# Attention in a written order: filler behind each bank of transposes, scan behind the transposes, value difference by halves

## The chip, the cores and the metric

The kernel runs on one core of one Trainium2 chip. A core has a matrix engine (TensorE, PE in the profile, with its weight loads shown as PEld), a vector engine (VectorE, DVE), a scalar engine (ScalarE, ACT), a general engine (GpSimd, POOL) and a queue for transfers (SyncE, SP). Each engine runs its own list of instructions in order and waits on semaphores for the others. Matmul results land in PSUM banks; everything else is kept in on-chip tiles, and larger tensors are sent to and fetched from memory by DMA. The metric is the device time of one execution in microseconds (us), as the median of several runs.

## The reference

One layer of a trunk with a parallel mixer: an input projection gives queries, keys and values for 16 heads of 64 columns, a gated convolution and two gates; then an output projection and a SwiGLU feed-forward part. Batch 1, 1024 tokens, 1024 columns, all in float32. The part around which the change turns is the attention, which has no softmax: weights come from a product of "not taken" probabilities over later keys.

```python
def stick_breaking_attention(q, k, v):
    """A[t,s] = sigmoid(z_ts) * prod_{s<j<t} (1 - sigmoid(z_tj)),  z = q.k / sqrt(Dh), s < t."""
    ...
    for i in range(s_len // Q_BLOCK):
        t0 = i * Q_BLOCK
        n_keys = t0 + Q_BLOCK
        qb = qh[:, :, t0:t0 + Q_BLOCK]
        kp = kh[:, :, :n_keys]
        vp = vh[:, :, :n_keys]
        z = jnp.einsum('bhqd,bhkd->bhqk', qb, kp) * inv_sqrt
        ...
        log_not = jnp.where(mask, jax.nn.log_sigmoid(-z), 0.0)
        excl = lax.cumsum(log_not, axis=3, reverse=True) - log_not
        log_a = jax.nn.log_sigmoid(z) + excl
        a = jnp.where(mask, jnp.exp(log_a), 0.0)
        outs.append(jnp.einsum('bhqk,bhkd->bhqd', a, vp))
```

## The kernel before

**Arithmetic.** Each float32 operand is split into a high part (a copy rounded to the matmul's format, made by ScalarE) and a low part (the rest, made by a VectorE subtract), and a product is three matmuls: high by high, high by low, low by high. So a weight `raw` becomes `whi` and `wlo`.

**The stages.** Norm and modulation, then the projections for keys, values, queries, convolution and gates (to about 567 us), then the attention stage (about 567 to 1030 us), the branch and output projections, and the feed-forward part. Outside the attention stage the change moves next to nothing.

**One step of the attention.** There are 16 heads with 8 query blocks each, 128 steps (h, i); step i sees (i+1) x 128 keys. Per step:

1. Scores: two matmuls per 512 keys into a bank `z` (two banks; lines 798 and 799). ScalarE takes the sigmoid into the tile `pt` (line 800; five `pt` tiles).
2. VectorE runs one scan over `pt` (line 804), which turns the sigmoids into running products from the last key back: 128 x (i+1) columns in one instruction.
3. Two steps later TensorE transposes `pt` in 128 x 128 blocks, up to four in a bank `tr` (three banks; line 819). ScalarE copies the bank to `ath` (line 822), and VectorE subtracts to get the low part `atl` (line 823), which frees the bank. A weight is the difference of two neighbouring running products; the kernel takes that difference on the value side instead, as told below.
4. For each pair of query blocks, three steps behind, the "av" matmuls multiply `ath` and `atl` by `vt` into the bank `o` (lines 834 and 835). ScalarE copies one half (`otmp`, line 839), VectorE adds the other (`oy`, line 841), SP sends it to `d_ya`.

`vt` of a head holds the differences of neighbouring value rows: `vb` and `va` (two loads of the same values, one row apart, for a pair of heads, `load_v`, line 748) are subtracted in `att_dv`, and the difference of a head is split into high and low. There is one buffer each of `va` and `vb`, so that the next pair can be loaded only once the difference has been taken (`va`) and split (`vb`).

**Fillers.** Attention does not keep TensorE busy by itself. The generator `fillers` brings other matmuls: first the second half of the value projection (256 columns each, lines 911 to 913, results copied to `vs` by ScalarE and written to `d_v`), 16 chunks of 24 matmuls; then two series of 16 chunks of 24 matmuls of 512 columns for the convolution branch (lines 892 to 894, in banks `pj`, of which there are two). Their VectorE and ScalarE work (`cy`, `ybl`, `mb`, and the weight splits `whi` and `wlo`) is issued with them.

**What sets the order.** `attention` yields after each part with a number that says how much filler the part is worth, and a loop at the end of the stage (functions below) issues filler up to that share. The first sixteen half chunks (`HEAD`) are written ahead of the attention, with the value projection's first half in them. The attention is traced at high priority; a scheduler then places each engine's instructions by its own estimate of when they can run, and `issue_after` keeps a filler behind the last score matmul. So neither TensorE's order nor VectorE's is the one in which the code is written: instructions of different steps pass each other.

## Time and profile before

| What | us |
|---|---|
| Median of 3 runs | 1842.04 (1841.74 to 1842.79) |
| Profiled execution | 1840.08 |
| Its span | 1838.3 |
| TensorE busy in the span | 1803.6 |
| VectorE busy | 1353.5 |
| ScalarE busy | 792.3 |

The span is the time from the first to the last instruction of the profiled execution. A profile's row for a group of instructions gives line, engine, operation, output and inputs, the count, then busy time in us and the mean of one in ns, then the engine's idle time just ahead of them and who ended it. A row of the waits gives engine, line, tile and whom it waited for, then the sum in us, the number of times and the longest. A row of the timeline gives the start in us, the duration, the engine and the instruction, and in brackets the idle time before it. A row of the windows gives the length of the window and then the busy time with the number of instructions for PE, PEld, DVE, ACT and POOL; after these come the clock granted to TensorE (1.00 is full speed), the share of the DMA engines and GB/s. Matmul ends are modelled and overlap the next one's start, so starts are what to compare.

### The profile page before, as it was taken

How to read it: one execution, taken by the hardware profiler on the slowest of the kernel's cores; microseconds unless marked ns; L12 is line 12 of the kernel's file. 1: busy time of each engine (PE TensorE's matmuls, PEld its weight loads, DVE VectorE, ACT ScalarE, POOL GpSimd, SP SyncE). 2: the span in 40 equal slices, each digit the busy share in tenths (PEclk: the TensorE clock that was granted, in tenths of full speed). 3: DMA queues.
4: the chain of work that ended last, by engine and by line, in shares of the span. 5: the costliest groups of instructions: out<-in, count | busy, mean ns of one | idle time of the engine just before them, and what ended most of it. 6: DMA issues, size and time to landing. Idle time of an engine off the chain costs nothing.

```text
span 1838.3 us, 24895 instructions
## 1 busy us (share of the span) xinstructions
PE 1803.6 (98%) x8829; PEld 1501.9 (82%) x8829; DVE 1353.5 (74%) x1949; ACT 792.3 (43%) x1494; POOL 366.4 (20%) x277
## 2 busy tenths in 40 slices
PE   7999999999999999999999999999999999999999
PEld 4787778888889988888888788877888888878887
DVE  7873776779874888888887644589877788644776
ACT  3452553333343656665665311664444344422321
POOL 0043327423240000000000000105544454200000
PEclk9999999999999999999999999999999999999999
DMA  9598452217748566588544636424533344299766
GB/s 395 198 317 303 162 188 76 86 70 260 275 157 265 153 183 180 178 240 278 153 133 141 209 126 209 142 92 161 195 138 147 130 172 170 103 340 334 283 228 221
DMA packets 147267, 358.01 MB, mean 195 GB/s; under 512 B 15480, under 2 KB 44480, under 8 KB 144968
## 3 DMA queue, kind: packets, MB, share of 16 engines
q1 hardware_dynamic: 101816, 289.12, 46.3%
q10 hardware_dynamic: 44320, 63.64, 9.9%
q0 software_dynamic: 1008, 3.67, 0.5%
q8 instruction: 70, 1.15, 0.3%
q14 instruction: 53, 0.43, 0.1%
HBM read 245.74 MB, written 110.66 MB: 194 GB/s over the span
## 4 chain that ended last, share of the span: by engine, by line
PE 76%; DVE 11%; DMA 6%; issue 3%; ACT 3%; POOL 0%; ACTq 0%; SPq 0%; DVEq 0%; POOLq 0%
PE e L131 6%; PE e L132 6%; PE e L133 6%; PE pj L131 5%; PE pj L133 5%; PE pj L132 5%; PE pj L308 5%; PE pj L892 4%; PE pj L893 4%; PE pj L894 4%; PE e L1427 4%; PE e L1426 4%; PE e L1428 4%; PE tr L819 3%; PE o L835 2%
## 5 line engine op out<-in xcount | busy, mean ns | idle before, releaser
L804 DVE TENSOR_TENSOR_SCAN pt<-pt,mk 128x128 f32<-128x128 f32 (+7 forms) x128 | 172.1, 1350 | 48.8 <-ACT pt L800 48.6
L800 ACT ACTIVATE pt<-z,rq 128x512 f32<-128x512 f32 (+3 forms) x192 | 107.3, 580 | 88.9 <-PE z L799 57.4
L131 PE MATMUL e<-big,whi 128*128 128x512 f32 x352 | 137.7, 391 | 1.9 <-ACT c L1326 1.9
L133 PE MATMUL e<-big,wlo 128*128 128x512 f32 x352 | 137.7, 391 | 0.0
L132 PE MATMUL e<-big,whi 128*128 128x512 f32 x352 | 137.6, 391 | 0.0
L136 DVE TENSOR_TENSOR c<-e,c 128x512 f32<-128x512 f32 x138 | 93.0, 687 | 56.0 <-PE e L133 55.0
L122 POOL TENSOR_SCALAR rs_m<-ss 128x1 f32<-128x1 f32 x8 | 1.5, 192 | 651.8 <-ACT xn L1229 651.8
L131 PE MATMUL pj<-big,whi 128*128 128x512 f32 x320 | 125.1, 391 | 0.5 <-DVE c L136 0.4
L132 PE MATMUL pj<-big,whi 128*128 128x512 f32 x320 | 124.7, 390 | 0.0
L133 PE MATMUL pj<-big,wlo 128*128 128x512 f32 x320 | 124.4, 390 | 0.0
L1426 PE MATMUL e<-whi,f 128*128 128x512 f32 (+1 forms) x319 | 121.7, 382 | 1.6 <-DMA f<-d_f 1.6
L1427 PE MATMUL e<-wlo,f 128*128 128x512 f32 (+1 forms) x319 | 121.8, 382 | 0.0
L1428 PE MATMUL e<-whi,f 128*128 128x512 f32 (+1 forms) x319 | 121.6, 382 | 0.0
L136 DVE TENSOR_TENSOR c<-pj,c 128x512 f32<-128x512 f32 x140 | 93.2, 682 | 27.3 <-PE pj L133 26.4
L136 DVE TENSOR_TENSOR wlo<-raw,whi 128x512 fp32r<-128x512 f32 x116 | 88.1, 763 | 34.2 <-ACT whi L489 34.1
L308 PE MATMUL pj<-whi,big 128*128 128x512 f32 x352 | 109.4, 396 | 3.7 <-ACT big L291 3.6
L489 ACT ACTIVATE whi<-raw 128x512 fp32r<-128x512 f32 x116 | 72.7, 631 | 89.1 <-PE pj L132 38.8
L823 DVE TENSOR_TENSOR atl<-tr,ath 128x512 fp32r<-128x512 f32 (+1 forms) x192 | 99.6, 548 | 14.4 <-ACT ath L822 12.6
L136 POOL TENSOR_TENSOR ws<-raw,raw 128x512 f32<-128x512 f32 x40 | 55.4, 1384 | 273.6 <-DMA raw<-w_cg 165.2
L822 ACT ACTIVATE ath<-tr 128x512 fp32r<-128x512 f32 (+1 forms) x192 | 86.9, 490 | 44.8 <-PE o L834 26.0
L132 PE MATMUL e<-rl,whi 128*128 128x512 f32 x264 | 103.6, 392 | 2.5 <-DVE rl L136 2.5
L892 PE MATMUL pj<-big,whi 128*128 128x512 f32 x256 | 103.9, 406 | 0.0
(258 smaller groups left out, 5015.9 us busy)
## 6 DMA issues: line engine op xcount, KB each, us to landing
f<-d_f SPq DMA_DIRECT2D x77, 512.0 KB, 3.6
d_f<-fs SPq DMA_DIRECT2D x70, 512.0 KB, 3.2
raw<-w_cg SPq DMA_DIRECT2D x40, 512.0 KB, 4.4
raw<-w_u SPq DMA_DIRECT2D x26, 512.0 KB, 3.2
raw<-w_g SPq DMA_DIRECT2D x25, 512.0 KB, 3.4
ad<-ada ACTq DMA_DIRECT2D x19, 512.0 KB, 5.0
ada<-ada SPq DMA_DIRECT2D x8, 1024.0 KB, 9.6
d_t<-ts SPq DMA_DIRECT2D x16, 512.0 KB, 4.0
```

The source lines that it names most:

```text
L131: nc.tensor.matmul(ps, wh[:, k, :], fh[:, k, :], start=(k == 0), stop=False)
L132: nc.tensor.matmul(ps, wh[:, k, :], fl[:, k, :], start=False, stop=False)
L133: nc.tensor.matmul(ps, wl[:, k, :], fh[:, k, :], start=False, stop=(k == 3))
L136: eng.tensor_tensor(out=out, in0=a, in1=b, op=op)
L308: nc.tensor.matmul(ps, a, b, start=(k == 0 and q == 0), stop=(k == KT - 1 and q == 2))
L800: nc.scalar.activation(pt[:, off + s0:off + s0 + m], z[:, :m], AF.Sigmoid, scale=rq[:, 1, i, h:h + 1])
L804: nc.vector.tensor_tensor_scan(out=pt[:, rev], data0=pt[:, rev], data1=mk[:, rev], initial=1.0, op0=ALU.mult, op1=ALU.max)
L823: nc.vector.tensor_tensor(out=tl[:, :nb, c0:c0 + P], in0=src, in1=th[:, :nb, c0:c0 + P].bitcast(F32), op=ALU.subtract)
L892: nc.tensor.matmul(ps, wh, rh_, start=(k == 0), stop=False)
L1426: nc.tensor.matmul(o, sh, w[0][:, c], start=(j == 0), stop=False)
L1427: nc.tensor.matmul(o, sh, w[1][:, c], start=False, stop=False)
L1428: nc.tensor.matmul(o, sl, w[0][:, c], start=False, stop=(j == NJ - 1))
```

## The change

In words:

- The attention's own VectorE instructions and all TensorE instructions from the start of the attention loop to the end of the fillers are chained: each gets a dependency on the one before it on its engine that is for the order alone. They then run as written. ScalarE, GpSimd, SP and the fillers' VectorE work are still placed by the scheduler.
- The amounts of filler are three numbers: `F_Z` behind a part of the scores, `F_T` for each transposed block, `F_O` behind av. A bank of four transposes is followed by filler, and av by none. Filler comes in pieces of one `k` (three matmuls, `KQ` 1) instead of two.
- The scan leaves `att_scores` and is issued after the transposes of two steps earlier. The av of a pair comes last in its step, save where the pair's second block is block 5: there it comes between the two banks of transposes.
- The value difference is taken for 64 columns of a head at a time: sixteen subtracts of 128 x 8 x 64 instead of eight of 128 x 8 x 128, one in step 3 (4 for every other head), the split two steps later.

The counts of instructions stay the same on TensorE, ScalarE, GpSimd and SP; VectorE gets eight more.

```diff
+    F_Z, F_T, F_O = 0.2,0.3,0
...
-    def att_dv(h):
+    def att_dv(h, part):
         va, vb = vab["va"], vab["vb"]
-        if h % 2 == 0:
-            tt(nc.vector, vb, vb, va, ALU.subtract)
-        dv = vb[:, :, h % 2 * DH:h % 2 * DH + DH]
+        cs = slice(h % 2 * DH, h % 2 * DH + DH)
+        dv = vb[:, :, cs]
+        if part == 0:
+            tt(nc.vector, dv, dv, va[:, :, cs], ALU.subtract)
+            return
...
             if s0 + m < n:
-                yield m / 512 * 0.43
+                yield F_Z
+        yield F_Z
+
+    def att_scan(h, i):
+        pt, off = ptof[h, i], D - (i + 1) * P
         rev = slice(D - 1, off - 1 if off else None, -1)
         nc.vector.tensor_tensor_scan(out=pt[:, rev], data0=pt[:, rev], data1=mk[:, rev], initial=1.0,
                                      op0=ALU.mult, op1=ALU.max)
-        yield m / 512 * 0.43
...
-            yield nb * 0.11
+            yield F_T * nb
...
-        yield (2 * g + 2) * 0.22
-
-    NZ, NTR, NPJ, DAV, KQ = 2, 3, 2, 3, 2
+        yield F_O
+
+    NZ, NTR, NPJ, DAV, KQ = 2, 3, 2, 3, 1
...
-                    if s == 2:
-                        att_dv(0)
-                    if s % 8 == (6 if h % 2 else 5) and h + 1 < H:
-                        att_dv(h + 1)
+                    if s in (1, 2):
+                        att_dv(0, s - 1)
+                    if s % 8 in ((4, 6) if h % 2 else (3, 5)) and h + 1 < H:
+                        att_dv(h + 1, s % 8 // 5)
...
                 yield from att_scores(h, i)
-            if s >= DAV:
-                h, i = steps[s - DAV]
-                if s % 2 != DAV % 2:
-                    yield from att_av(h, i // 2)
-            if 0 <= s - 2 < len(steps):
-                yield from att_trans(*steps[s - 2])
+            tr_ = att_trans(*steps[s - 2]) if 0 <= s - 2 < len(steps) else iter(())
+            av_ = att_av(steps[s - DAV][0], steps[s - DAV][1] // 2) if s >= DAV and s % 2 != DAV % 2 else iter(())
+            yield from itertools.islice(tr_, 1)
+            if s >= DAV and steps[s - DAV][1] == 5:
+                yield from av_
+            yield from tr_
+            if s < len(steps):
+                att_scan(*steps[s])
+            yield from av_
...
-    ATT = sum((i + 1) * 0.2175 + (i % 2) * (i + 1) * 0.22 for i in range(8)) * H
+    ATT = sum(F_Z * (1 + i // 4) + F_T * (i + 1) + F_O * (i % 2) for i in range(8)) * H
...
+    pe, mine = len(nc.cur_bb.bb.instructions), set()
     while True:
+        n0 = len(nc.cur_bb.bb.instructions)
         with tc.high_priority():
             ca_ = next(at_, None)
+        mine.update(i.name for i in nc.cur_bb.bb.instructions[n0:])
...
+    prev = {}
+    for i in nc.cur_bb.bb.instructions[pe:]:
+        if i.engine == nc.tensor.engine or i.name in mine and i.engine in (nc.vector.engine,):
+            if i.engine in prev:
+                tc.add_manual_dep(i, prev[i.engine].name, mybir.DependencyInfo(mybir.DependencyClass.NoSync, mybir.DependencyReason.DATA),
+                                  reason="in_order")
+            prev[i.engine] = i
```

Three places show what moves. A row gives a number, the line, the operation, and output and inputs with the output's size; `SCALAR_TENSOR_TENSOR` is the scan. First VectorE in the middle of the stage, in a head of before that the prediction speaks of (the scan of step 4, of 640 columns, and what stands round it):

```order
803 L936 TENSOR_TENSOR ybl_7076<-cy_6983,ybh_7075 128x512
804 L136 TENSOR_TENSOR wlo_7540<-raw_7537,whi_7539 128x512
805 L804 SCALAR_TENSOR_TENSOR pt_4844<-pt_4844,mk 128x640
806 L823 TENSOR_TENSOR atl_7008<-tr_7009,ath_7007 128x3x128
807 L823 TENSOR_TENSOR atl_7008<-tr_7027,ath_7007 128x4x128
808 L823 TENSOR_TENSOR atl_7082<-tr_7083,ath_7081 128x128
809 L841 TENSOR_TENSOR oy_6968<-o_6954,otmp_6967 64x256
810 L804 SCALAR_TENSOR_TENSOR pt_4845<-pt_4845,mk 128x768
```

The same part of a head in the changed kernel:

```order
876 L831 TENSOR_TENSOR atl_7695<-tr_7729,ath_7694 128x2x128
877 L813 SCALAR_TENSOR_TENSOR pt_4844<-pt_4844,mk 128x512
878 L831 TENSOR_TENSOR atl_7750<-tr_7751,ath_7749 128x3x128
879 L813 SCALAR_TENSOR_TENSOR pt_4845<-pt_4845,mk 128x640
880 L849 TENSOR_TENSOR oy_7767<-o_7761,otmp_7766 64x256
881 L137 TENSOR_TENSOR vt_7772<-vb_7216,vt_7772 128x8x64
882 L831 TENSOR_TENSOR atl_7750<-tr_7783,ath_7749 128x4x128
883 L813 SCALAR_TENSOR_TENSOR pt_4841<-pt_4841,mk 128x768
```

Before, three banks' subtracts stand in a row behind the scan of step 4; now the subtracts of a step and a scan take turns. TensorE at the same place before, with the three runs of transposes that follow each other:

```order
3417 L799 MATMUL z_7143<-skl_6643,sqt_6641 128x512
3418 L798 MATMUL z_7147<-skh_6642,sqt_6641 128x256
3419 L799 MATMUL z_7147<-skl_6643,sqt_6641 128x256
3420 L819 MATMUL tr_7092<-dm,pt_4841 128x128 x2
3421 L819 MATMUL tr_7128<-dm,pt_4842 128x128 x3
3422 L819 MATMUL tr_7152<-dm,pt_4843 128x128 x4
3423 L798 MATMUL z_7164<-skh_6642,sqt_6641 128x512
```

And in the changed kernel:

```order
3651 L827 MATMUL tr_7783<-dm,pt_4844 128x128 x4
3652 L903 MATMUL pj_7682<-big_148,whi_7676 128x512
3653 L904 MATMUL pj_7682<-big_217,whi_7676 128x512
3654 L905 MATMUL pj_7682<-big_148,wlo_7677 128x512
3655 L903 MATMUL pj_7682<-big_148,whi_7676 128x512
3656 L904 MATMUL pj_7682<-big_217,whi_7676 128x512
3657 L905 MATMUL pj_7682<-big_148,wlo_7677 128x512
3658 L803 MATMUL z_7799<-skh_7269,sqt_7268 128x512
3659 L804 MATMUL z_7799<-skl_7270,sqt_7268 128x512
3660 L803 MATMUL z_7803<-skh_7269,sqt_7268 128x384
3661 L804 MATMUL z_7803<-skl_7270,sqt_7268 128x384
3662 L827 MATMUL tr_7809<-dm,pt_4845 128x128 x4
```

Each bank of transposes now has filler between it and the next. Last, TensorE at the beginning of the attention, where the fillers are the value projection (`pj` from 911 to 913) and the scores are those of steps 0 and 1. Before:

```order
2398 L798 MATMUL z_5117<-skh_4860,sqt_4859 128x128
2399 L798 MATMUL z_5155<-skh_4860,sqt_4859 128x256
2400 L911 MATMUL pj_4976<-whi_4888,big_148 128x256
2401 L912 MATMUL pj_4976<-wlo_4889,big_148 128x256
2402 L913 MATMUL pj_4976<-whi_4888,big_217 128x256
2403 L911 MATMUL pj_4976<-whi_4888,big_148 128x256
2404 L799 MATMUL z_5117<-skl_4861,sqt_4859 128x128
2405 L799 MATMUL z_5155<-skl_4861,sqt_4859 128x256
```

In the changed kernel the scores of step 0 stand at the same place, and then, 116 rows later:

```order
2512 L923 MATMUL pj_5141<-wlo_5128,big_148 128x256
2513 L924 MATMUL pj_5141<-whi_5127,big_217 128x256
2514 L803 MATMUL z_5156<-skh_4860,sqt_4859 128x256
2515 L804 MATMUL z_5156<-skl_4861,sqt_4859 128x256
2516 L803 MATMUL z_5164<-skh_4860,sqt_4859 128x384
2517 L804 MATMUL z_5164<-skl_4861,sqt_4859 128x384
2518 L827 MATMUL tr_5170<-dm,pt_4842 128x128
2519 L803 MATMUL z_5185<-skh_4860,sqt_4859 128x512
2520 L804 MATMUL z_5185<-skl_4861,sqt_4859 128x512
```

Between them stand only matmuls of the value projection: the scores of step 1 have moved behind the whole first half and half a chunk of the second.

More of the change, by code (lines that the diff above doesn't have):

```diff
@@ L1 @@
+import itertools
 from contextlib import ExitStack
```

## The prediction

> **What bounds the kernel now.** I read the page first: the busy time of each engine and the chain that ended last.
>
> ```profile
> PE 1803.6 (98%) x8829; PEld 1501.9 (82%) x8829; DVE 1353.5 (74%) x1949; ACT 792.3 (43%) x1494; POOL 366.4 (20%) x277
> PE 76%; DVE 11%; DMA 6%; issue 3%; ACT 3%; POOL 0%; ACTq 0%; SPq 0%; DVEq 0%; POOLq 0%
> ```
>
> TensorE (PE) is the bound. The change issues as many matmuls as before and reorders them only in the attention stage (about 567 to 1030 us). So it can win only what TensorE loses to waits there. The stage by windows, the waits in it, and the two groups of waiting matmuls:
>
> ```profile
> 720.00:760.00 40.00, 38.93 (x236) 33.66 (x235) 35.15 (x48) 26.45 (x60) 0.00 (x0) 1.00 0.43 124
> ACT pt L800 <- PE z L799: 57.4, 58, 2.7
> ...
> PE tr L819 <- DVE atl L823: 5.4, 11, 0.8
> ...
> DVE vb L136 <- DMA vb<-d_v: 3.2, 4, 1.6
> ...
> PE o L834 <- DVE oy L841: 0.8, 5, 0.2
> L819 PE MATMUL tr<-dm,pt 128*128 128x128 f32 x576 | 97.8, 273 | 5.8 <-DVE atl L823 5.4 <-DVE pt L804 0.4
> ```
>
> In the first line TensorE is busy 38.93 of 40 us at a granted clock of 1.00, VectorE (DVE) 35.15. ScalarE's long waits for `z` cost nothing; TensorE's own are 5.4 + 0.8 + 0.4 = 6.6 us in 17 waits. One of them, seen on both engines:
>
> ```profile
> 746.99 0.28 PE L798 MATMUL z<-skh,sqt 128*128 128x256 f32 x1
> 747.11 0.28 PE L799 MATMUL z<-skl,sqt 128*128 128x256 f32 x1
> 748.21 0.44 PE L819 MATMUL tr<-dm,pt 128*128 128x128 f32 x2 [0.82 <-DVE atl L823]
> 748.90 0.84 PE L819 MATMUL tr<-dm,pt 128*128 128x128 f32 x6 [0.25 <-DVE atl L823]
> 745.20 0.69 DVE L136 TENSOR_TENSOR wlo<-raw,whi 128x512 fp32r<-128x512 f32 x1 [0.37 <-ACT whi L489]
> 746.07 1.49 DVE L804 TENSOR_TENSOR_SCAN pt<-pt,mk 128x640 f32<-128x640 f32 x1 [0.18 <-ACT pt L800]
> 747.59 1.35 DVE L823 TENSOR_TENSOR atl<-tr,ath 128x384 fp32r<-128x384 f32 x3
> ```
>
> All three `tr` banks are full. Their subtracts stand on VectorE behind a weight split and the 1.49 us scan, run from 747.59, and only then may the next transposes start at 748.21. The page's idle time is too small: a 256-column matmul is shown as 0.28 us though its successor starts 0.12 us later (746.99 to 747.11), so each wait costs 0.16 us more than the idle shown (747.11 to 748.21 is 1.10, less 0.12 is 0.98, against 0.82). The loss is 6.6 + 17 x 0.16 = 9.3 us. At the end of the stage, where the branch projection needs the last attention outputs:
>
> ```profile
> PE pj L892 <- ACT ya L1037: 0.5, 1, 0.5
> ...
> PE pj L893 <- DVE ya L136: 0.2, 1, 0.2
> PE pj L892 <- DVE mb L964: 0.2, 1, 0.2
> ```
>
> That is 0.9 + 3 x 0.16 = 1.4 us. So nothing above 10.7 us, 0.6%, is to be had.
>
> **The change, part by part.** *Scan behind the transposes, a fixed VectorE order, filler behind each bank.* On VectorE the subtracts of step s-2 now come ahead of the scan of step s, so a full bank no longer waits for a scan issued after it; on TensorE nine transposes in a row (2, 3 and 4) become single banks with three or six filler matmuls behind each. What could be late instead is the scan for its own transposes, two steps later. I add up the tightest places from these rows (and the scan's 1.49 above):
>
> ```profile
> 743.88 0.39 PE L892 MATMUL pj<-big,whi 128*128 128x512 f32 x1
> ...
> 744.57 0.71 PE L819 MATMUL tr<-dm,pt 128*128 128x128 f32 x5
> 745.03 0.36 PE L834 MATMUL o<-ath,vt 128*128 128x256 f32 x1
> L823 DVE TENSOR_TENSOR atl<-tr,ath 128x384 fp32r<-128x384 f32 x32 | 17.6, 549 | 9.3 <-ACT ath L822 8.8 <-PE o L835 0.2
> L822 ACT ACTIVATE ath<-tr 128x384 fp32r<-128x384 f32 x32 | 15.7, 492 | 16.8 <-PE o L834 13.5 <-PE tr L819 1.4
> L136 DVE TENSOR_TENSOR vt<-vb,vt 128x512 fp32r<-128x512 f32 x16 | 10.7, 677 | 0.1
> L136 DVE TENSOR_TENSOR vb<-vb,va 128x1024 f32<-128x1024 f32 x8 | 9.7, 1216 | 3.2 <-DMA vb<-d_v 3.2
> ```
>
> A filler of three matmuls takes 0.69 us (743.88 to 744.57), so 0.23 each; a transpose 0.11 (0.46 us for the five, whose last hands 0.08 on to the next matmul). From the last score matmul of step 4 to that step's first transposes TensorE does: filler 0.69, three transposes 0.33, filler 0.69, the av of blocks 0 and 1 (two matmuls of 256 and two of 128 columns) 0.41, scores of step 5 0.70, four transposes 0.44, two fillers 1.38, scores of step 6 0.81: 5.45 us. Meanwhile the three transposes end at about 1.2 (0.69 + 0.33, shown 0.16 longer), ScalarE's copy at 1.7 (0.49), the subtract at 2.3 (0.55), the scan at 3.8 (1.49): 1.6 us to spare. The same sum gives 1.4 us for step 3 and 1.8 to 3.0 for steps 5, 6, 7 and 0. Per head VectorE has 21.9 us of work, TensorE 25. So I expect the 9.3 us to go, and next in line is the second half of the scores, which needs a `z` bank back from ScalarE: about 0.1 us short once a head in the same sum; I leave that within rounding (16 x 0.1 = 1.6 us) and use it in the range.
>
> *Value difference halved.* Eight instructions of 1.216 us become sixteen of the size of the `vt` split, 0.677: 16 x 0.68 - 8 x 1.22 = +1.1 us of VectorE. It lies in the 3 us per head that VectorE has over. Its loads' waits (3.2 us in total) lay under TensorE's work before; now the pair is free three steps earlier, and the loads have about six steps, 20 us. Cost 0.
>
> *The start.* Here the written order takes cover away. Before, TensorE put the scores of steps 1 to 4 and some of their transposes between the matmuls of the value projection. Now only step 0 stands there, and step 1 comes after all of the first half and half a chunk of the second. What that covered:
>
> ```profile
> L912 PE MATMUL pj<-wlo,big 128*128 128x256 f32 x19 | 5.3, 282 | 0.0
> L913 PE MATMUL pj<-whi,big 128*128 128x256 f32 x19 | 5.3, 281 | 0.0
> L911 PE MATMUL pj<-whi,big 128*128 128x256 f32 x18 | 5.2, 291 | 0.0
> ...
> 578.90 0.40 PE L798 MATMUL z<-skh,sqt 128*128 128x128 f32 x2
> ...
> 579.09 3.84 SPq L916 DMA_DIRECT2D d_v<-vs  x3
> ...
> 588.33 0.39 ACT L915 ACTIVATE vs<-pj 128x256 f32<-128x256 f32 x1 [2.58 <-DMA d_v<-vs]
> 588.77 0.38 PE L911 MATMUL pj<-whi,big 128*128 128x256 f32 x1
> ```
>
> (The first three rows are the projection's matmuls from 578.9 to 588.75.) The fifth chunk's copy on ScalarE waits for the first write of `d_v` to land, issued at 579.09 behind the next head's loads on the SP queue; until 588.77 the seventh chunk has no `pj` bank. In those 9.87 us the projection fills 56 x 0.12 = 6.7 us and attention 3.15. Without attention, save step 0's 0.25, TensorE stands idle for 2.9 us. The writes ahead in the SP queue are the same, so the landing should not move; the weights' loads for the second half stand a little earlier in that queue, since a 512 KB value load moves behind them: no cost. The first steps then come with hardly any filler between:
>
> ```profile
> L800 ACT ACTIVATE pt<-z,rq 128x256 f32<-128x256 f32 x32 | 15.1, 473 | 9.4 <-PE z L799 9.4
> L804 DVE TENSOR_TENSOR_SCAN pt<-pt,mk 128x256 f32<-128x256 f32 x16 | 10.8, 678 | 1.1 <-ACT pt L800 1.1
> ```
>
> From the start of step 1's scores TensorE has 0.24 + 0.35 + 0.11 = 0.70 us of work before step 3's scores, which need the first `z` bank back: 0.40 for the scores as shown, 0.47 for the sigmoid and some 0.15 to pass it on make 1.0, 0.3 us of waiting; and the transposes of step 1 wait another 0.3 us for its scan (0.9 + 0.68 + 0.15 = 1.75 against 1.0 + 0.46). I take 0.6 us. Bounds: 0 (the write lands earlier) and 4.5 us (everything attention covered, 3.15, and twice 0.6).
>
> Such an idle time has an echo in this trace:
>
> ```profile
> 1231.06 0.80 PE L132 MATMUL e<-rl,whi 128*128 128x512 f32 x1 [2.49 <-DVE rl L136]
> 1228.00:1232.00 4.00, 1.49 (x4) 1.02 (x4) 4.00 (x6) 3.00 (x4) 0.00 (x0) 0.85 0.10 41
> 1232.00:1236.00 4.00, 4.00 (x14) 3.13 (x13) 4.00 (x8) 2.31 (x4) 0.00 (x0) 0.72 0.27 86
> 174.00:182.00 8.00, 5.73 (x27) 4.40 (x26) 3.04 (x7) 4.38 (x8) 5.04 (x4) 1.00 1.06 392
> ```
>
> After 2.49 us idle the granted clock fell to 0.85 and 0.72 over two windows of 4 us: 0.15 x 4 + 0.28 x 4 = 1.7 us lost. An interrupted stretch at 174 to 182 (5.73 of 8 busy) kept 1.00. An idle time of 2.9 us is nearer to the first, so I charge 1.7 us; bounds 0 and 1.7. The Trainium skill, "TensorE: Matmul & The Clock Gate", Part 1, says that the clock halves after at least one idle window of about 3.4 us; the 2.49 us above were less and drew it, so here the measurement decides. By the page's rule this term would be 0 and the sum -6.9.
>
> *The end of the stage.* Fifteen filler matmuls of the last merged chunk instead of six now stand between the last av and the rest, and more of the first output half's projection after them: 9 x 0.23 = 2.1 us more for the last waits, each of which was 0.5 us idle at most. I take 1.1 of the 1.4 us; bounds 0 and 1.4.
>
> *Elsewhere.* Outside the stage VectorE, ScalarE and GpSimd swap single neighbours in the feed-forward part: 0, between -1 and +1.
>
> Sum: -9.3 - 1.1 + 2.9 + 0.6 + 1.7 = -5.2 us. The profiled execution took 1840.08 us (span 1838.3) and would take 1834.9; it lies 1.96 us below the median of the runs, 1842.04, so I forecast a median of 1836.8.
>
> **The rivals.** *No loss at the start*, or part of it: the clock stays up (-6.9, so 1835.1), or the bank comes in time as well (-9.3 - 1.1 + 0.6 = -9.8, so 1832.2). For it speaks the stretch at 174 us, and for the first form the page of the Trainium skill named above; against it, that the landing of the write is set by loads that do not change.
>
> *The waits only change place* (same): ScalarE's turn. The `z` banks are the tight spot, and a weight split at the head of ScalarE's queue waits for TensorE to give up the old weights before a sigmoid may run. At 0.33 us per head it gives 16 x 0.33 = 5.3 us back and nothing is left: 1842. Against it: in ScalarE's new order each such split follows the copy of transposes that TensorE issues within three matmuls of the old weights' last reader, so it waits about 0.4 us.
>
> *Slower:* a fixed order means that VectorE can't run past a late instruction. The place is the value difference in steps 3 and 4: with its load late, everything behind it (subtract, scan) is late too, and TensorE, in fixed order as well, can't put filler first. The row above shows 3.2 us of such waits in 4 places, 1.6 at most. A wait of W us costs W - 1.4 once the 1.4 us of slack are used up; over the eight pairs of heads it must exceed 1.4 + 5.2/8 = 2.05 us to cancel the gain, and at 2.5 us it gives 8 x 1.1 = 8.8 us, so 1842.04 + 3.6 = 1845.6. Against it: loads that start earlier.
>
> **How the numbers follow.** The forecast (1836.8, its own range 1834 to 1839.5 from the `z` bank's 1.6 us, the tail's 1.1 and the outside's 1) gets 0.45; a smaller loss at the start (1832 to 1835) 0.22; waits that change place (1839 to 1844) 0.16; slower 0.17. The range goes from 1831.5, just under the best case, to 1845.5, about where the slower rival stands: it leaves out under 2 in 10. About 0.2%, 3.7 us, is what a measurement of this kernel can tell from no change: faster means below 1838.4. That takes all of the small-loss case, 0.41 of the forecast's 0.45 and a little of the third: 0.64; within 0.2% 0.19; slower, above 1845.7 or near it with the third case's tail, 0.17.
>
> **What would show it.** In the changed profile: TensorE's waits on `atl` from 600 to 1000 us near 0 (right) or replaced by waits on `pt` from VectorE or ScalarE (wrong); TensorE idle for about 3 us just before 588.8, with or without a stretch of half clock behind it; the first waits on `ya` at the end gone; VectorE's waits on the value loads no longer than 1.4 us. The forecast is wrong if VectorE, once its order is fixed, turns out to fall behind TensorE by more than the 1.4 to 3 us counted here.

## The result and the profile after

The changed kernel takes 1836.9 us (median of 7 runs, 1832.49 to 1838.48) against 1842.44 us for the kernel before, run with it. The ratio is 0.996 with a 95% interval of 0.9946 to 0.9975: faster by 4.6 to 9.9 us. The forecast was 1836.8.

The profiled execution has a span of 1835.0 us, 3.3 us less than before. The page's first rows and the chain that ended last:

```profile
PE 1802.3 (98%) x8829; PEld 1503.8 (82%) x8829; DVE 1353.1 (74%) x1957; ACT 794.9 (43%) x1494; POOL 366.7 (20%) x277
PE 85%; DVE 6%; DMA 5%; issue 2%; ACT 1%; POOL 1%; SPq 0%; ACTq 0%; DVEq 0%; POOLq 0%
```

The chain runs over TensorE for 85% of the span instead of 76%, and over VectorE for 6% instead of 11%. By windows, the start of the attention, a stretch in the middle, and its end:

```profile
587.00:600.00 13.00, 9.98 (x71) 9.78 (x71) 0.56 (x2) 2.64 (x6) 0.00 (x0) 0.87 1.04 311
720.00:760.00 40.00, 40.00 (x248) 35.31 (x247) 36.42 (x54) 25.71 (x60) 0.00 (x0) 1.00 0.66 192
1000.00:1030.00 30.00, 28.65 (x138) 23.64 (x137) 16.81 (x28) 11.23 (x21) 0.00 (x0) 1.00 0.73 237
```

The middle, 38.93 of 40 us busy before, is full. The start has a hole of 3 us and a lower clock, and the end is no better than it was. TensorE's own waits between 575 and 1030 us, from the view of the waits:

```profile
PE pj L922 <- ACT vs L926: 3.0, 1, 3.0
...
PE pj L903 <- ACT ya L1058: 1.3, 1, 1.3
...
PE z L803 <- ACT pt L805: 0.2, 1, 0.2
```

The eleven waits on `atl` and the five on `oy` are gone; three waits are left. The first of them on the timeline:

```profile
590.19 0.28 PE L923 MATMUL pj<-wlo,big 128*128 128x256 f32 x1
590.31 0.28 PE L924 MATMUL pj<-whi,big 128*128 128x256 f32 x1
593.61 0.58 PE L922 MATMUL pj<-whi,big 128*128 128x256 f32 x1 [3.02 <-ACT vs L926]
593.98 0.42 PE L923 MATMUL pj<-wlo,big 128*128 128x256 f32 x1
594.20 0.42 PE L924 MATMUL pj<-whi,big 128*128 128x256 f32 x1
593.17 0.66 ACT L926 ACTIVATE vs<-pj 128x256 f32<-128x256 f32 x2 [5.34 <-DMA d_v<-vs]
```

This is the idle time that the prediction named: ScalarE's copy waits for the first write of `d_v` to land, and TensorE waits for the copy. Behind it the matmuls of 256 columns follow each other at 0.22 us (593.98 to 594.20) instead of 0.12 us.

**Where the time went.** TensorE has the same instructions outside the attention stage, in the same order, so I take the same two matmuls in both traces, one shortly before the value projection and one in the branch projection (rows of before, then of after):

```profile
541.31 0.39 PE L131 MATMUL pj<-big,whi 128*128 128x512 f32 x1
...
1050.42 0.39 PE L894 MATMUL pj<-ya,wlo 128*128 128x512 f32 x1
```

```profile
546.14 0.39 PE L132 MATMUL pj<-big,whi 128*128 128x512 f32 x1
...
1050.30 0.39 PE L905 MATMUL pj<-ya,wlo 128*128 128x512 f32 x1
```

Between them lie 509.1 us before and 504.2 us after: the stage got 4.9 us shorter. What comes ahead got 4.8 us longer (541.31 to 546.14), and what follows 3.1 us shorter (784.74 us from the second matmul to the end of the span, instead of 787.85). The part ahead has the same instructions in the same order on every engine. In this execution a load of `uu` came late, VectorE waited for it, TensorE after VectorE, and the clock fell. From the changed kernel's timeline of VectorE and its windows:

```profile
508.23 1.23 DVE L554 CUSTOM_DVE_ANT_0 uu<-uu,cab 128x1024 f32<-128x1024 f32 x1 [2.01 <-DMA uu<-ada]
516.00:520.00 4.00, 2.35 (x7) 1.90 (x8) 4.00 (x8) 1.87 (x4) 0.00 (x0) 0.80 0.68 224
520.00:524.00 4.00, 4.00 (x15) 3.17 (x15) 2.57 (x5) 1.89 (x4) 0.91 (x1) 0.77 0.69 237
```

Over the fourteen profiles of this case the part ahead lasts from 541.3 to 547.6 us, and the one of before has the shortest. So the stage's own length is what the experiments below compare ("the stage"; their expectations place the first matmul in the value projection, it stands a little ahead of it). Within the stage the traces of two kernels agree to some hundredths of a microsecond wherever nothing was changed.

### The profile page after: what moved, and what is told of

It is laid out like the page before. It is cut to its first block, busy times and chain, and to the rows that moved or that the text cites. A ratio compares the mean times of both kernels' runs of the same rounds, so it can differ in the third digit from the quotient of the medians.

```text
span 1835.0 us, 24920 instructions
## 1 busy us (share of the span) xinstructions
PE 1802.3 (98%) x8829; PEld 1503.8 (82%) x8829; DVE 1353.1 (74%) x1957; ACT 794.9 (43%) x1494; POOL 366.7 (20%) x277
## 4 chain that ended last, share of the span: by engine, by line
PE 85%; DVE 6%; DMA 5%; issue 2%; ACT 1%; POOL 1%; SPq 0%; ACTq 0%; DVEq 0%; POOLq 0%
PE e L132 7%; PE e L134 7%; PE e L133 7%; PE pj L132 5%; PE pj L134 5%; PE pj L133 5%; PE pj L309 5%; PE pj L903 5%; PE pj L905 5%; PE pj L904 5%; PE e L1447 4%; PE e L1449 4%; PE e L1448 4%; PE tr L827 3%; PE o L843 2%; PE z L803 2%
## 5 line engine op out<-in xcount | busy, mean ns | idle before, releaser
L132 PE MATMUL pj<-big,whi 128*128 128x512 f32 x320 | 125.2, 391 | 1.7 <-DVE c L137 1.7
L133 PE MATMUL pj<-big,whi 128*128 128x512 f32 x320 | 124.8, 390 | 0.0
L831 DVE TENSOR_TENSOR atl<-tr,ath 128x512 fp32r<-128x512 f32 (+1 forms) x192 | 103.9, 551 | 19.1 <-ACT ath L830 17.6
L805 ACT ACTIVATE pt<-z,rq 128x512 f32<-128x512 f32 (+1 forms) x192 | 104.8, 575 | 27.2 <-PE z L804 27.1
L903 PE MATMUL pj<-big,whi 128*128 128x512 f32 x256 | 114.0, 445 | 0.0
L830 ACT ACTIVATE ath<-tr 128x512 fp32r<-128x512 f32 (+1 forms) x192 | 93.2, 487 | 30.3 <-PE tr L827 29.4
```

Source lines behind the costliest of these rows:

```text
L132: nc.tensor.matmul(ps, wh[:, k, :], fh[:, k, :], start=(k == 0), stop=False)
L133: nc.tensor.matmul(ps, wh[:, k, :], fl[:, k, :], start=False, stop=False)
L805: nc.scalar.activation(pt[:, off + s0:off + s0 + m], z[:, :m], AF.Sigmoid, scale=rq[:, 1, i, h:h + 1])
L831: nc.vector.tensor_tensor(out=tl[:, :nb, c0:c0 + P], in0=src, in1=th[:, :nb, c0:c0 + P].bitcast(F32), op=ALU.subtract)
L903: nc.tensor.matmul(ps, wh, rh_, start=(k == 0), stop=False)
```

## The experiments

Each kernel is the changed one with the edit shown. "Ratio" is against the kernel before, run on the same chip. The stage is read from one profiled execution each.

| Run | Stage, us | Median, us | Ratio (95% interval) |
|---|---|---|---|
| before | 509.1 | 1842.4 | |
| changed | 504.2 | 1836.9 | 0.996 (0.9946 to 0.9975) |
| e1: start left to the scheduler | 499.1 | 1832.4 | 0.9934 (0.9921 to 0.9947) |
| e2: scan behind the scores | 516.1 | 1847.4 | 1.0018 (1.0005 to 1.0032) |
| e3: no fixed order | 505.5 | 1839.5 | 0.997 (0.996 to 0.9981) |
| e4: value difference whole | 507.3 | 1838.3 | 0.9967 (0.9951 to 0.9983) |
| e5: fixed order on TensorE alone | 516.7 | 1849.4 | 1.0035 (1.0023 to 1.0047) |
| e6: fixed order on VectorE alone | 522.2 | 1852.5 | 1.0048 (1.0031 to 1.0066) |
| e7: filler behind the scores alone | 522.7 | 1852.7 | 1.0046 (1.0029 to 1.0063) |
| e8: output weights' split later | 504.4 | 1835.9 | 0.9958 (0.9941 to 0.9974) |
| e9: more matmuls in the idle time | 506.6 | 1843.0 (one run) | |
| e10: e1 and e8 together | 498.4 | 1830.4 | 0.993 (0.9912 to 0.9947) |
| e11: other buffers for three copies | 500.9 | 1832.4 | 0.9942 (0.9922 to 0.9963) |
| e12: amounts of filler as before | 514.2 | 1846.4 | 1.0019 (1.0004 to 1.0033) |

### The start

**e1, the written order from step 5 on:**

```diff
             flush[0] = s >= len(steps)
+            if s == 5:
+                first[0] = len(nc.cur_bb.bb.instructions)
...
-    pe, mine = len(nc.cur_bb.bb.instructions), set()
+    first, mine = [None], set()
...
-    for i in nc.cur_bb.bb.instructions[pe:]:
+    for i in nc.cur_bb.bb.instructions[first[0]:]:
```

> The written order begins only with step 5; steps 0 to 4 are placed by the scheduler as before. My theory (the gain is the lost waits for the subtracts, the loss is the attention that no longer covers the value projection's copies at the start): TensorE's idle time of 3.2 us ahead of the seventh chunk and the stretch of lower clock behind it go, together with some 0.8 us of thin filler, and the steady part stays without waits. Measured from the same matmul of the value projection to the same one of the branch projection, the stage takes 509.1 us before and 504.2 us in the change; here 499 to 500, and the median about 1832. Rival (the idle time is set by the write of d_v alone and comes at another place): the stage stays within 1 us of 504.2.

Measured: stage 499.1 us, 5.1 us shorter. The window at the start and one in the middle:

```profile
587.00:600.00 13.00, 12.48 (x102) 12.10 (x101) 7.98 (x12) 7.05 (x16) 0.00 (x0) 1.00 1.06 360
...
720.00:760.00 40.00, 40.00 (x244) 35.00 (x243) 37.04 (x53) 27.57 (x63) 0.00 (x0) 1.00 0.55 160
```

TensorE is busy 12.48 of 13 us instead of 9.98, at a clock of 1.00. Matmul by matmul, the lead over the changed kernel is 4.95 us after the start and stays 4.95 us to the end of the attention. So the loss lay at the start alone. The fixed order is worth keeping behind it: with no fixed order at all (e3, below) the stage takes 505.5 us, 6.4 us more than here.

**e11, other buffers for three of the first copies,** taken from a ring that attention needs only later:

```diff
-                vs = fq.tile([P, 256], F32, tag=("ybh", "ybl")[i % 2], bufs=2, name=nm("vs1"))
+                vs = (fq.tile([P, 256], F32, tag=("ybh", "ybl")[i % 2], bufs=2, name=nm("vs1")) if e or not 4 <= i < 7 else
+                      bp.tile([P, 4, 256], F32R, tag="atl", bufs=3, name=nm("vs1"))[:, 0].bitcast(F32))
```

> Three of the first half's chunk copies get other buffers, so that the fifth copy need not wait for the first write of d_v to land; written order as in the change. If the idle time of 3.2 us comes from that buffer: none ahead of the seventh chunk and no lower clock; then the second half's weights, loaded when they were, are next in line with 0.5 to 1.5 us of waiting. Stage 500.5 to 502. If the write only shows up there and the matmuls wait for something else: within 1 us of 504.2.

Measured: stage 500.9 us, no idle time ahead of the seventh chunk. In its place stand short waits, as this view of the waits shows:

```profile
PE z L803 <- ACT pt L805: 0.6, 2, 0.4
...
PE pj L923 <- DVE wlo L137: 0.3, 1, 0.3
```

So it was the buffer of that copy, whose write had not landed, that held TensorE; and the second half's weights were indeed next in line, with 0.3 us (0.5 to 1.5 expected).

**e9, work in the idle time:**

```diff
+                if e == 0 and i == 6:
+                    wt_ = pps.tile([P, 512], F32, tag="tr", bufs=NTR, name=nm("warm"))
+                    for r in range(26):
+                        nc.tensor.matmul(wt_[:, :256], hh[1][:, r % KT, :P], w[3][0][:, :256], start=(r == 0), stop=(r == 25))
                 ps = ps_f()[:, :256]
```

> The change with 26 matmuls of 256 columns more, written into a bank that nobody reads, ahead of the seventh chunk of the value projection: 26 x 0.12 = 3.1 us of work in the idle time of 3.2 us, which itself stays. If the idle time drew the lower clock (granted clock 0.87 from 587 to 600 us): no such stretch, the seventh chunk at a pitch of 0.12 us from its first matmul, stage 1.4 us shorter than 504.2, so 502.8. If the stretch of lower clock comes from something else: stage 504.2 plus or minus 0.4, with the stretch still there.

Measured: the lower clock is gone. The windows from 590 to 610 us, and the first matmul of the seventh chunk and a later one on the timeline:

```profile
590.00:600.00 10.00, 9.31 (x78) 9.11 (x77) 0.00 (x0) 1.38 (x5) 0.00 (x0) 1.00 1.03 306
600.00:610.00 10.00, 9.59 (x71) 8.56 (x70) 8.13 (x13) 7.76 (x18) 0.00 (x0) 1.00 0.82 251
595.87 0.38 PE L926 MATMUL pj<-whi,big 128*128 128x256 f32 x1 [0.69 <-ACT vs L930]
...
596.92 0.28 PE L928 MATMUL pj<-whi,big 128*128 128x256 f32 x1
```

The chunk and the first matmul behind it take 2.97 us from start to start; in the changed kernel the same stretch takes 4.42 us (24 x 0.12 = 2.88 at full clock). So the idle time drew the lower clock, and the clock cost 1.5 us. The stage as a whole was not 1.4 us shorter, as expected, but 2.4 us longer: the write landed 0.8 us later than in the changed kernel's profile, and the end of the stage lost 3.0 us more, where TensorE waited 2.7 us for a copy of `ya` (1.3 us in the changed kernel) and the clock fell again (0.83 from 1018 to 1028 us). Up to there it was 0.6 us ahead.

The landing varies: in the seven runs that have the written order at the start, the old buffers and no added matmuls, the idle time cost 3.2 to 4.05 us, and the 24 matmuls behind it took 4.4 to 5.3 us. In e2, e5 and e7 a few matmuls more ran at the lower clock, so that it cost 1.5 to 2.8 us in all. The start of the changed kernel may thus cost up to 1.9 us more than in its own profile. The granted clock was 0.50 from 594 to 596 us in the changed kernel. From 590 to 605 us it was 0.89 there and 0.77 in the other six, which at half clock is some 3.3 and 6.9 us (an estimate from these windows). The Trainium skill, "TensorE: Matmul & The Clock Gate", Part 1, says that the full clock returns after about one busy window of 3.4 us, whose phase is free-running: the first fits one such window, the others two.

### The steady part

**e2, the scan back right behind the scores:**

```diff
                 yield from att_scores(h, i)
+                att_scan(h, i)
...
             yield from tr_
-            if s < len(steps):
-                att_scan(*steps[s])
             yield from av_
```

> Only the scan goes back to its place right behind the scores; both engines keep the written order, and the filler stays behind each bank. My theory: the subtracts of a step stand behind the scan again, now in every head and with nothing allowed past, so that the second bank's transposes wait in steps 4 to 7: at least 0.5 us per head, stage 512 or more, waits of TensorE on atl or a z bank from 600 to 1000 us above 5 us. Rival (the filler behind each bank gives the subtracts time enough, the scan's place doesn't matter): stage 504 plus or minus 1.

Measured: stage 516.1 us, 11.9 us longer; 7 us longer than before the change. Of the 11.9 us, 9.5 lie behind 615 us; the other 2.4 come at the start, most of them because the write of `d_v` landed later. The waits from 615 to 1000 us, then one of them on VectorE and on TensorE:

```profile
PE o L843 <- DVE atl L831: 5.8, 8, 1.5
...
746.76 2.28 DVE L813 TENSOR_TENSOR_SCAN pt<-pt,mk 128x1024 f32<-128x1024 f32 x1
749.07 0.69 DVE L942 TENSOR_TENSOR cy<-pj,cy 128x512 f32<-128x512 f32 x1
749.68 0.68 DVE L831 TENSOR_TENSOR atl<-tr,ath 128x512 fp32r<-128x512 f32 x1
749.23 0.28 PE L842 MATMUL o<-ath,vt 128*128 128x256 f32 x1
750.41 0.38 PE L843 MATMUL o<-atl,vt 128*128 128x256 f32 x1 [0.91 <-DVE atl L831]
```

The subtract stands behind the longest scan again (and a filler's `cy`), but it is not the next transposes that wait, as I had expected first of all, but the av matmul that reads this `atl`. With both orders fixed, the scan's place decides; filler behind the banks does not make up for it.

**e3, no fixed order; e5 and e6, on one engine only:**

```diff
-        if i.engine == nc.tensor.engine or i.name in mine and i.engine in (nc.vector.engine,):
+        if False:
```

```diff
-        if i.engine == nc.tensor.engine or i.name in mine and i.engine in (nc.vector.engine,):
+        if i.engine == nc.tensor.engine:
```

```diff
-        if i.engine == nc.tensor.engine or i.name in mine and i.engine in (nc.vector.engine,):
+        if i.name in mine and i.engine in (nc.vector.engine,):
```

> Everything of the change but the fixed order on TensorE and VectorE: the scheduler places all. My theory: the order as written is what keeps subtracts and scans taking turns; without it part of the waits on atl comes back, and the start is covered again: stage 501 to 507. Rival (the new code and the new amounts of filler carry the gain, the fixed order adds only the loss at the start): no waits on atl, stage 499 to 500.

> The fixed order on TensorE alone; VectorE is placed by the scheduler. My theory (VectorE's alternation of subtracts and scan is what counts, and the scheduler gives it as well when the code is written in that order): waits on atl under 1 us, stage within 1 us of 504.2. Rival (VectorE's fixed order is needed): the scheduler puts scans ahead of subtracts, TensorE can't go around, stage 508 or more.

> The fixed order on VectorE alone; TensorE is placed by the scheduler, so attention covers the start again. My theory: the start's 4 to 5 us come back, and the steady part keeps few waits since the subtracts come first: stage 499 to 503. Rival (the filler behind each bank exists only in TensorE's fixed order; without it the transposes pile up again): waits on atl of 3 us or more, stage 503 to 508.

Measured: 505.5, 516.7 and 522.2 us. Without any fixed order (e3) the start is 4.5 us better than in the changed kernel, and the rest loses 5.8 us, so that the net is 1.3 us worse: the size that my theory gave, but not for its reason. One wait on `atl` from 615 to 1000 us, and one at the end of the stage:

```profile
PE tr L827 <- DVE atl L831: 0.8, 1, 0.8
...
PE pj L903 <- DVE mb L975: 2.5, 1, 2.5
```

Of the 5.8 us, 2.8 come behind the last av, where TensorE waits 2.5 us for `mb` and the clock falls (0.83 from 1012 to 1022 us). Only 3.0 us come in the steady part, and the waits on `atl` are 0.8 us of them. So the rest of the change, left to the scheduler, keeps about two thirds of what the steady part gained. Either order alone is worse than the kernel before, and my theory for each fell; e6 lies outside its rival's range too. From e5's timeline of VectorE and its waits from 615 to 1000 us:

```profile
744.63 2.28 DVE L813 TENSOR_TENSOR_SCAN pt<-pt,mk 128x1024 f32<-128x1024 f32 x1
746.94 0.69 DVE L943 TENSOR_TENSOR cy<-pj,cy 128x512 f32<-128x512 f32 x1
747.55 0.68 DVE L831 TENSOR_TENSOR atl<-tr,ath 128x512 fp32r<-128x512 f32 x1
...
PE o L843 <- DVE atl L831: 4.6, 10, 0.8
PE z L803 <- ACT pt L805: 0.6, 1, 0.6
```

Though the code has the scan behind the transposes, the scheduler puts it ahead of the subtracts, as in e2, and TensorE, in its fixed order, waits at the same place. In e6 it is the other way round. Its waits from 615 to 1000 us:

```profile
PE tr L827 <- DVE pt L813: 6.5, 10, 0.8
...
PE o L842 <- DVE oy L849: 4.8, 5, 2.2
```

Here VectorE takes things in order, and the scheduler puts TensorE's transposes where their scan is not done.

**e7 and e12, other amounts of filler:**

```diff
-    F_Z, F_T, F_O = 0.2,0.3,0
+    F_Z, F_T, F_O = 0.9,0,0
```

```diff
-                yield F_Z
-        yield F_Z
+                yield m / 512 * 0.43
+        yield m / 512 * 0.43
...
-            yield F_T * nb
+            yield nb * 0.11
...
-        yield F_O
+        yield (2 * g + 2) * 0.22
...
-    ATT = sum(F_Z * (1 + i // 4) + F_T * (i + 1) + F_O * (i % 2) for i in range(8)) * H
+    ATT = sum((i + 1) * 0.2175 + (i % 2) * (i + 1) * 0.22 for i in range(8)) * H
```

> The filler comes behind the scores alone, none behind the transposes (the three numbers 0.9, 0 and 0); fixed order and scan as in the change. My theory: two banks of transposes in a row are within the three banks, but the second step's have to wait for the subtracts of the first; some 0.3 us per head, stage 507 to 511. Rival (the scan behind the transposes is enough): stage 504 plus or minus 1.

> The change with the amounts of filler of the kernel before: in proportion to TensorE's own time of each part, scores 0.43 per 512 keys, transposes 0.11 per block, av 0.44 per pair of blocks (so most of the filler comes behind the scores and the av, and little behind the transposes); fixed orders, scan and pieces of three matmuls as in the change. The run with filler behind the scores alone also gave light steps as much filler as heavy ones, so it mixed two things; this one doesn't. If filler behind each bank of transposes is what lets the subtracts keep up: stage 508 to 516. If the fixed orders and the scan's place carry the gain and only the even spread over light and heavy steps was wrong in that run: 504.2 plus or minus 1.

Measured: 522.7 and 514.2 us. e7 is far beyond the 507 to 511 us of my theory; of its 18.5 us, some 11 come from the last head on, and its light steps get as much filler as its heavy ones, so its size says little. e12 changes the amounts alone: with the filler in proportion to TensorE's own work, both fixed orders and the scan in place, the stage is 10 us longer than in the change, 9.6 of them in the steady part. The waits from 615 to 1000 us:

```profile
PEld o L843 <- DVE atl L831: 5.6, 11, 1.4
PE o L843 <- DVE atl L831: 3.0, 7, 1.2
```

Again av waits for a subtract. So with both orders held the gain needs the scan behind the subtracts and the filler behind the banks together; with one order held it is lost; with none, most of the steady part's gain stays. Which of scan and filler counts without a fixed order has not been tested. Two parts of the change have no run of their own: the smaller pieces of filler (`KQ` 1) and the place of av in its step.

**e4, the value difference whole:**

```diff
         if part == 0:
-            tt(nc.vector, dv, dv, va[:, :, cs], ALU.subtract)
+            if h % 2 == 0:
+                tt(nc.vector, vb, vb, va, ALU.subtract)
             return
```

> The value difference is taken whole again, for both heads of a pair in one instruction of 1.2 us, in the fixed order. My theory: it lies in the 3 us per head that VectorE has over: stage within 0.5 us of 504.2. Rival (in a fixed order a long instruction ahead of the subtracts costs its excess of 0.54 us in every second head): 8 x 0.54 = 4.3 us, stage 508.

Measured: 507.3 us, 3.1 us longer. Of this 1.1 us lie at the start, where the write of `d_v` landed 0.6 us later; the other 2.0 us come in small steps over the heads, 0.25 us for a pair. The waits from 615 to 1000 us:

```profile
PEld z L804 <- ACT pt L806: 3.1, 9, 0.5
```

Between my 0 and the rival's 4.3 us: the excess is partly covered, and what is not shows as a wait for a `z` bank, the place that the prediction called tight. How the longer subtract reaches ScalarE's sigmoid, I haven't followed.

### The end

**e8, the split of the first output weights behind the copies of `ya`:**

```diff
-            nc.scalar.activation(h_, yr, AF.Copy)
+            last_ya = nc.scalar.activation(h_, yr, AF.Copy)
...
-            preload_wo()
+            with tc.issue_after(last_ya.ins):
+                preload_wo()
```

The reason for it, from the changed kernel's timeline of ScalarE and TensorE:

```profile
1010.88 1.16 ACT L1043 ACTIVATE whi<-raw 128x512 fp32r<-128x512 f32 x2 [5.35 <-DMA raw<-w_o]
...
1016.29 1.15 ACT L1043 ACTIVATE whi<-raw 128x512 fp32r<-128x512 f32 x2 [2.18 <-DMA raw<-w_o]
1018.39 0.61 ACT L1058 ACTIVATE ya<-yr 128x512 fp32r<-128x512 f32 x1
1019.12 0.47 PE L903 MATMUL pj<-ya,whi 128*128 128x512 f32 x1 [1.35 <-ACT ya L1058]
```

> The split of the output projection's first weights is put behind the last copy of ya on ScalarE. My theory for the tail, where I had forecast 1.1 us of gain and none came: ScalarE stands 5.4 and 2.2 us at that split, waiting for its load, with copies of ya behind it, and TensorE's 1.5 us of waiting at the end of the stage go: stage 502.5 to 503. Rival (the load of yr itself is late, whatever stands ahead): within 0.4 us of 504.2.

Measured: the stage is 504.4 us, within the rival's range and not the 502.5 to 503 us of my theory. But its start was 1.3 us longer, since the write of `d_v` landed 0.5 us later and the clock stayed down longer. At its end it won 1.1 us back: the wait on `ya` is gone, and TensorE's longest wait there is 0.2 us. So the theory holds for the end, and the number fell to the start. The median can't tell it from the changed kernel's (1835.9 against 1836.9).

**e10, e1 and e8 together** (no other edit):

> The written order from step 5 on, and the output projection's first weight splits behind the copies of ya. The two gains lie at the two ends of the stage and should add up: stage 498 to 499, median about 1831. If one of them is only moved to another wait, 499.5 to 502.

Measured: stage 498.4 us, median 1830.4 us, ratio 0.993 (0.9912 to 0.9947): 10.7 us of stage less than before, and the fastest of all. Against e1 it wins 1.2 us at the end and loses 0.4 us at the start, which the edit leaves as in e1. In the stage the two gains add up; between e10 and e1 the medians of whole executions (1830.4 and 1832.4, on different chips) show no difference that their intervals would bear.

## Why the prediction was right

The stage came out as forecast, and most of the terms with it. That the median met the forecast to 0.1 us is luck: its interval alone spans 5.3 us, and in the two profiles the parts ahead of the stage and behind it moved by +4.8 and -3.1 us, so that the profiled execution, forecast at 1834.9 us, took 1836.9. By terms of the sum, in us, from the two profiles:

| Step | Forecast | Measured |
|---|---|---|
| Waits of the steady part | -9.3 | -9.7 (17 starts in the steady part with 9.2, one at 603.3 with 0.5) |
| Idle time ahead of the seventh chunk | +2.9 | +3.2 |
| Lower clock behind it | +1.7 | +1.5 |
| First steps with thin filler | +0.6 | +1.0 |
| End of the stage | -1.1 | 0.0 (1.5 lost before and after) |
| Small differences, none over 0.25 | | -0.9 |
| Stage | -5.2 | -4.9 |

- **Waits of the steady part:** right, and for the reason given. From 632 us to the end of the attention no matmul of the changed kernel loses more than 0.25 us. e2 shows that in a fixed order the scan's place decides, e12 that the filler behind the banks is needed as well; e3 shows that the fixed order itself is worth 3.0 us of it. What I had not seen is how narrow this is: I named the transposes as the ones that would be late, with 1.4 us and more to spare, while in e2, e5 and e12 it is av that waits for its subtract. The margins I added up were not the smallest ones.
- **The start:** right in cause and close in size. e11 shows the buffer, e1 the cover that is missing, e9 the clock. The lower clock was taken from the trace of before, against the window that the Trainium skill's page gives ("TensorE: Matmul & The Clock Gate", Part 1), and it came. One row was misread on the way: the window from 174 to 182 us, called an interrupted stretch, holds a single idle time of 2.27 us that kept the full clock. An idle time of that length draws the lower clock in some profiles and not in others (last section), so 1.7 us was less sure than the sum makes it look; at the start, with 3.0 to 3.9 us idle, it came in all seven profiles. The upper bound of 4.5 us for the first steps should be 4.35 by its own terms; nothing rests on it.
- **Value difference, "cost 0":** mis-sized as a statement. e4 shows that halving is worth about 2.0 us of the stage; the whole instruction would not have been free in a fixed order. Since the forecast was for halves, the sum was not hurt.
- **The end, "I take 1.1 of the 1.4 us":** this step failed: 1.1 us was forecast, 0.0 came. I had moved the last waits by the filler ahead of them and had not asked what ScalarE does in the meantime. It stood 5.4 and 2.2 us at a weight split, and `ya` came late by the same 1.5 us. e8 takes the split away and wins 1.1 us.
- **Elsewhere, "0, between -1 and +1":** mis-sized; in the two profiles +4.8 us ahead of the stage and -3.1 us behind it. The first I put down to variation, since every engine's order is the same there. Behind it, all thirteen profiles of changed kernels have 784.3 to 787.2 us, under the 787.85 us of before. From 1240 to 1280 us nine instructions on VectorE, four on ScalarE and one on GpSimd stand at another place, more than the single neighbours that the prediction names. But 2.8 of the 3.1 us come ahead of them: TensorE's wait near 1231 us is 1.45 instead of 2.49 us, and no lower clock follows it. With one profile of before, what of this is the change's doing stays open. The medians say that the whole is more than the stage: in each of the twelve kernels that have a ratio, the median stands better against before than the stage does, by 0.4 to 4.1 us, 2.2 on average.
- **The rivals:** "no loss at the start" is what e1 built, at 1832.4 us against the 1832.2 us that I had worked out for it. "Slower by a late load" did not happen: in the change VectorE waited for a value load once, 0.9 us. "The waits only change place" did not happen in the change. In e2, e5, e6 and e12, each 10 us or more longer in the stage than the change, waits did change place, but for the most part to `atl`, to VectorE's `pt` and to `oy`, and not to the `z` banks that the rival named.

## What to carry to other kernels

An order written out by hand has to be held on all engines that trade waits: on TensorE or VectorE alone it was slower than the scheduler's order of the same code (516.7 and 522.2 against 505.5 us). On both it gave 504.2 us, and 499.1 where the start was left out of it. It also takes away cover that nobody wrote down: look at each place where the scheduler had filled a wait for a transfer, here the first steps of attention in the value projection, and leave that part out of the written order. When a wait is to be pushed out by more work ahead of it, look first at what stands ahead of the awaited instruction on its own engine.

## What was not expected of the hardware

An idle time of TensorE of 2 to 3 us can cost more than itself: 2.49 us idle before, 3.0 us by the profile at the start of the changed kernel and 2.1 us in its projections (the windows from 516 to 524 us above) were each followed by a stretch of lower clock that cost 1.5 to 1.7 us, and up to 2.8 us at the start of the experiments. It need not: all fourteen profiles have an idle time ahead of the same matmul near 180 us. Before, then in the changed kernel:

```profile
180.27 0.50 PE L131 MATMUL pj<-ft,whi 128*128 128x512 f32 x1 [2.27 <-ACT whi L489]
178.00:190.00 12.00, 9.73 (x44) 8.04 (x44) 4.19 (x6) 4.12 (x8) 5.20 (x5) 1.00 0.62 231
```

```profile
180.03 0.50 PE L132 MATMUL pj<-ft,whi 128*128 128x512 f32 x1 [2.26 <-ACT whi L490]
178.00:190.00 12.00, 9.97 (x37) 8.09 (x38) 4.59 (x6) 3.75 (x8) 5.15 (x5) 0.86 0.61 225
```

The clock in this window is 0.86 in ten profiles and 1.00 in four, among these e8 with 3.25 us idle. What decides, no run here shows. And whole executions of one kernel differ by more than the change gains: eleven of the kernel before on one chip took 1839.0 to 1850.2 us. A stage that is bound by TensorE repeats to some hundredths of a microsecond meanwhile. Where I followed a difference between profiles, it lay in the landing of single transfers and in the clock behind the idle times that they cause.
